# Two columns instead of four in the first phase of a decoder layer: sums kept in PSUM, eight ada_w buffers, the norm's root inside the modulation

## The chip, the cores and the metric

The kernel runs on one core of a Trainium2 chip. A core has five engines that run their own instruction queues and wait for each other by semaphores: TensorE (PE in the profile, its weight loads PEld), VectorE (DVE), ScalarE (ACT), GpSimd (POOL) and SyncE (SP), which issues the transfers here. The metric is the device time of one execution in microseconds.

## The reference

One layer of a hybrid decoder on 1024 prompt tokens and 64 sample tokens (8 sequences of 8), model width 2048, float32. The change concerns the first lines of the layer: the modulation is computed from the condition vectors `c` (nine rows: one prompt, eight samples), the input is normalised, scaled and shifted, and projected.

```python
mod = jax.nn.silu(c.astype(f32)) @ ada_w.astype(f32) + ada_b.astype(f32)
shift, scale, gate = jnp.split(mod, 3, axis=-1)
h = (_rmsnorm(x, norm_g).astype(f32) * (1.0 + scale[:, None]) + shift[:, None]).astype(dt)
proj = h @ w_in
...
vn = _rmsnorm(v_b, sgu_g)
```

`_rmsnorm` multiplies by the reciprocal root of the mean square over the 2048 features of a token. `v_b` is four columns of 128 of the projection ("vb" below). What follows (dilated attention, a spatial-gating MLP, an mLSTM, an output projection, a gated residual) is not touched.

## The kernel before

Everything lies transposed: a tile is 128 features (partitions) by 1088 tokens. There are 16 feature tiles `xs[k]`, and a column of the projection is 128 outputs by all tokens, summed over the 16 feature tiles. Tokens are cut into three chunks `CH` of 384, 384 and 320 columns, so that a product fits one PSUM bank.

Float32 products are made of three float32r products: a high and a low half of the activation (`hH`, `hL`) and of the weight (`wh`, `wl`): `hH*wh + hL*wh + hH*wl` (function `products`, lines 252 to 254). The weight's halves are made by `Weights`: SP loads `wraw`, ACT rounds it to `wh` (L98), POOL subtracts (L99). Those of a feature tile are made by `modulate` (x times scale plus shift on DVE, L420 to L424; ACT rounds it to `hH`, L425) and `modulate_low` (`hL`, L431). Before that `scaled` has multiplied x by the root `rbc` of its token (L398, on DVE for the first two tiles, on POOL for the others).

The scale and shift come from ada_w, 2048 by 6144, read in the same phase. PE multiplies it with the nine condition vectors: a group `g` of 4 MB (eight transfers of 512 KB) gives scale and shift of two feature tiles, in four sets of matmuls (`ada_set`, L342); the four row strips of the result are copied by ACT (L366, `ada_sum`), turned by PE transposes (L374, `ada_turn`) and summed by DVE (L376), and `modulation` makes scale and shift of it (L409 to L411). Group 0 is cut in two halves (`ada_half`, L353), one for each feature tile, so that the first tile comes early. Groups 8 to 11 make the gate of the residual later.

The order is written out by hand. Instructions stand in each engine's queue in the order in which Python issues them; generators such as `ada_group` are stepped between the products by tables of steps (`AT`). Buffers come from pools with a fixed number of turns. The first phase computes the four vb columns (`NST = 4`): for each feature tile or pair of tiles, the products of all four columns go to PSUM, and are added to `accs` in SBUF (by ACT's copy for the first tile, by DVE after that, L553 and L584). ada_w has four buffers of 512 KB (`ad`), of which a set takes two. Then comes the gate column (two 32-wide strips for the mLSTM's gates, L632 to L636), and from there `column` computes one column after the other, all 16 feature tiles in a row, with its sums in three PSUM banks.

PSUM has eight banks: four for products (`mm`), four for everything else (`bgp`, through `bank`).

## Time and profile before

| | us |
|---|---|
| median of three runs | 2462.2 (2461.33 to 2462.92) |
| the profiled execution | 2462.13 |
| its span in the profile | 2460.1 |
| PE busy in the span | 2419.0 |
| first vb product (its hL part) starts | 49.4 |
| gate column starts (vb columns done on PE) | 198.5 |
| DMA moved in the first 320 us, GB/s | 230 |

The profile is one execution; times in it are from the span's start. A row of the timeline has start, duration, engine, line, operation, output and inputs by their names in the program, shapes, and in brackets how long the engine was idle before it and who released it. A row of a group has the count, then busy us and the mean in ns. A row of stages has the stretch, its length, busy us and number of instructions of PE, PEld, DVE, ACT and POOL, the granted clock of PE (1.00 is full), the mean share of the DMA engines and GB/s.

### The profile page before, as it was taken

The page shows a single profiled execution, that of the slowest core. Times are in us where ns is not written, and L with a number is a line of the kernel's source. Part 1 is how long each engine was busy: PE and PEld are TensorE (multiplying, and loading weights), DVE is VectorE, ACT ScalarE, POOL GpSimd, SP SyncE. Part 2 cuts the span into 40 slices and gives each one's busy share as a digit, 9 for nine tenths or more (in the row PEclk, how much of TensorE's full clock was granted, in tenths as well). Part 3 has the DMA queues.
Part 4 walks back from the last instruction along what each step waited for, and adds up shares of the span by engine and source line. Part 5 has one row for each costly group of instructions (what it writes and reads, how often), then busy time and mean ns, then how long its engine had stood idle before and what let it go on. Part 6 is the DMA issues. An engine that isn't in the chain of part 4 may idle for free.

```text
span 2460.1 us, 39820 instructions
## 1 busy us (share of the span) xinstructions
PE 2419.0 (98%) x15879; PEld 2237.5 (91%) x15879; DVE 923.8 (38%) x2489; ACT 746.1 (30%) x1638; POOL 644.3 (26%) x502
## 2 busy tenths in 40 slices
PE   5899999999999999999999999999999999999999
PEld 2677899999999999999999999888989999999898
DVE  5662300323232231323352001333311688887322
ACT  3222221323323232323321111222212566666210
POOL 2431222232322232222221322121211333332321
PEclk8999999999999999999999999999999999999999
DMA  8774621111121112112411524657565855554454
GB/s 289 255 258 158 220 65 44 57 62 57 54 65 58 53 49 73 38 52 71 127 56 59 172 76 171 223 178 265 188 240 187 255 157 165 152 151 139 164 171 141
DMA packets 157081, 332.95 MB, mean 135 GB/s; under 512 B 21770, under 2 KB 76834, under 8 KB 149216
## 3 DMA queue, kind: packets, MB, share of 16 engines
q1 hardware_dynamic: 156896, 330.41, 41.1%
q8 instruction: 125, 2.05, 0.3%
q14 instruction: 60, 0.49, 0.1%
HBM read 284.26 MB, written 54.55 MB: 138 GB/s over the span
## 4 chain that ended last, share of the span: by engine, by line
PE 95%; DMA 2%; DVE 2%; issue 0%; SPq 0%; ACT 0%; POOL 0%; DVEq 0%; POOLq 0%; ACTq 0%
PE mm L252 27%; PE mm L254 26%; PE mm L253 26%; PE pt L1493 2%; PE ad L342 2%; PE os L1300 1%; PE o L1504 1%; PE sq L1250 1%; PE o L1502 1%; DMA ad<-in_adaw 1%; PE s L1452 1%; PE s L1451 1%; DMA x<-in_xT 1%; PE b L942 0%; PE b L974 0%; PE b L982 0%
## 5 line engine op out<-in xcount | busy, mean ns | idle before, releaser
L252 PE MATMUL mm<-hH,wh 128*128 128x384 f32 (+1 forms) x3168 | 1058.5, 334 | 9.3 <-ACT hH L425 8.1
L253 PE MATMUL mm<-hL,wh 128*128 128x384 f32 (+1 forms) x3168 | 1034.8, 327 | 2.6 <-DVE hL L431 2.6
L254 PE MATMUL mm<-hH,wl 128*128 128x384 f32 (+1 forms) x3168 | 1036.0, 327 | 0.0
L99 POOL TENSOR_TENSOR wl<-wraw,wh 128x512 fp32r<-128x512 f32 x344 | 445.7, 1304 | 1545.8 <-ACT wh L98 1433.4
L252 PEld LDWEIGHTS mm<-hH,wh 128*128 128x128 f32 x3168 | 595.9, 188 | 51.3 <-issue 32.1
L253 PEld LDWEIGHTS mm<-hL,wh 128*128 128x128 f32 x3168 | 596.3, 188 | 4.4 <-DVE hL L431 3.6
L254 PEld LDWEIGHTS mm<-hH,wl 128*128 128x128 f32 x3168 | 595.4, 188 | 0.0
L98 ACT CAST wh<-wraw 128x512 fp32r<-128x512 f32 x344 | 200.8, 596 | 409.6 <-PE mm L253 270.9
L252 PE MATMUL mm<-yH,wh 128*128 128x512 f32 (+2 forms) x768 | 261.7, 341 | 0.0
L254 PE MATMUL mm<-yH,wl 128*128 128x512 f32 (+2 forms) x768 | 251.7, 328 | 0.4 <-POOL wl L99 0.4
L253 PE MATMUL mm<-yL,wh 128*128 128x512 f32 (+2 forms) x768 | 251.7, 328 | 0.0
L254 PEld LDWEIGHTS mm<-yH,wl 128*128 128x128 f32 x768 | 144.8, 189 | 11.7 <-POOL wl L99 0.9
L252 PEld LDWEIGHTS mm<-yH,wh 128*128 128x128 f32 x768 | 145.1, 189 | 9.6
L253 PEld LDWEIGHTS mm<-yL,wh 128*128 128x128 f32 x768 | 145.3, 189 | 9.3
L898 DVE SCALAR_TENSOR_TENSOR u<-R,cw,u 128x384 f32<-128x384 f32 (+1 forms) x108 | 62.0, 574 | 213.3 <-ACT u L896 210.8
L1588 DVE SCALAR_TENSOR_TENSOR xo<-mm,gate,xo 128x512 f32<-128x512 f32 (+2 forms) x96 | 54.5, 569 | 117.4 <-PE mm L254 101.8
L1494 ACT CAST pH<-pt 128x512 fp32r<-128x512 f32 (+1 forms) x120 | 65.3, 544 | 63.3 <-PE pt L1493 62.5
L1495 DVE TENSOR_TENSOR pL<-pt,pH 128x512 fp32r<-128x512 f32 (+1 forms) x120 | 74.8, 623 | 11.6 <-ACT pH L1494 11.2
L1463 ACT ACTIVATE P<-P,mx 128x128 f32<-128x128 f32 (+3 forms) x96 | 74.4, 777 | 1.0 <-DVE mx L1460 1.0
L1493 PE MATMUL pt<-cst,P 128*128 128x128 f32 x432 | 66.6, 272 | 0.0
L1454 DVE CUSTOM_DVE_ANT_0 P<-s,btab 128x384 f32<-128x384 f32 (+2 forms) x96 | 54.7, 570 | 30.0 <-PE s L1452 29.1
L1504 PE MATMUL o<-pL,vh 128*64 128x256 f32 x240 | 61.8, 281 | 1.9 <-DVE pL L1495 1.9
(324 smaller groups left out, 2378.8 us busy)
## 6 DMA issues: line engine op xcount, KB each, us to landing
wraw<-in_win SPq DMA_DIRECT2D x264, 256.0 KB
ad<-in_adaw SPq DMA_DIRECT2D x96, 512.0 KB
kv<-in_ck SPq DMA_DIRECT2D x30, 1024.0 KB
kv<-in_cv SPq DMA_DIRECT2D x30, 1024.0 KB
wraw<-in_wout SPq DMA_DIRECT2D x48, 256.0 KB
x<-in_xT SPq DMA_DIRECT2D x16, 544.0 KB
yraw<-yD SPq DMA_DIRECT2D x16, 544.0 KB
xo<-in_xT SPq DMA_DIRECT2D x16, 544.0 KB
```

The lines of the kernel that those rows point to most:

```text
L98: self.nc.scalar.copy(wh[:, :n], raw[:, :n])
L99: self.nc.gpsimd.tensor_tensor(wl[:, :n], raw[:, :n], wh[:, :n].bitcast(FT), op=OP.subtract)
L252: T.matmul(ps[:, :n], wh[:, a], rh[:, t0:t0 + n], start=first and i == 0, stop=False)
L253: T.matmul(ps[:, :n], wh[:, a], rl[:, t0:t0 + n], start=False, stop=False)
L254: T.matmul(ps[:, :n], wl[:, a], rh[:, t0:t0 + n], start=False, stop=last and i == len(rows) - 1)
L898: V.scalar_tensor_tensor(u[:, :npr], R[:, j:j + npr], cw[:, m, j:j + 1], u[:, :npr], op0=OP.mult, op1=OP.add)
L1454: V.tensor_tensor_reduce(s[:, k0:k0 + w], ps[:, :w], e["bt"][:, x:x + w], 1.0, mx[:, np_ - 1:np_] if np_ else -3.0e38, op0=OP.add, op1=OP.max,
L1463: S.activation(s[:, :nk], s[:, :nk], AF.Exp, bias=mx[:, 2:3], accum_out=mx[:, 3:4])
L1493: T.transpose(pt[:, o:o + 128], P[r][:, k:k + 128], ident)
L1494: S.copy(pH[:, f:], pt[:, f:])
L1495: at(0, 3, lambda: V.tensor_tensor(pL[:, f:], pt[:, f:], pH[:, f:].bitcast(FT), op=OP.subtract))
L1504: T.matmul(po[0][0:64, :256], e["vh"][:, kb, 0, :], pL[:, c], start=False, stop=(kb == 2 * m + 1), skip_group_check=True)
```

## The change

The first phase now computes only the first two vb columns (`NST = 2`). Their sums over all 16 feature tiles stay in six PSUM banks (two columns by three chunks); the two other banks serve `ad` and `at`. At the end ACT copies the six sums out (`h_vb`), and the other two vb columns are computed by `column` behind the phase, with the gate column after them. ada_w has eight buffers in the phase. Groups 0 and 1 are both cut into halves, so tiles 0 to 3 come one by one, each chunk by chunk; group 2 is stepped in tile 3, and from then group g+1 in the products of group g. The multiplication by the root is gone as a step: `modulate` multiplies x by scale and root in one three-operand instruction on DVE, ACT adds the shift as it rounds to `hH`, and `modulate_low` adds the shift again on DVE as it subtracts. The first weight tile's low half is made by DVE instead of POOL.

```diff
 def bank(name="bg"):
+    if start:
+        tag = "bg" if name in ("ad", "at") else "acc"
+        return bgp.tile([128, 512], FT, tag=tag, name=name, bufs=2 if tag == "bg" else 6)
     return bgp.tile([128, 512], FT, tag="bg", name=name, bufs=4)
...
-    NST = 4
+    NST = 2
...
+    def ahead():
+        ada_dma(used[0] + (8 if start else 4))
...
-        V.tensor_scalar(x[:, a], x[:, a], md[:, 1, 0:1], md[:, 0, 0:1], op0=OP.mult, op1=OP.add)
+        V.scalar_tensor_tensor(x[:, a], x[:, a], md[:, 1, 0:1], rbc[:, a], op0=OP.mult, op1=OP.mult)
+        S.activation(hH[k][:, a], x[:, a], AF.Identity, bias=md[:, 0, 0:1])
         if t1 == TOK:
...
+            V.tensor_tensor(x[:, NPR:], x[:, NPR:], rbc[:, NPR:], op=OP.mult)
...
-        S.copy(hH[k][:, t0:t1], x[:, t0:t1])
+            S.copy(hH[k][:, NPR:], x[:, NPR:])
...
-        eng.tensor_tensor(hL[k][:, t0:t1], xs[k][:, t0:t1], hH[k][:, t0:t1].bitcast(FT), op=OP.subtract)
+        V.scalar_tensor_tensor(hL[k][:, a], xs[k][:, a], md[:, 0, 0:1], hH[k][:, a].bitcast(FT), op0=OP.add,
+                               op1=OP.subtract)
...
+    accs = [[bank("mm") for c in range(3)] for j in range(NST)]
+    for k in range(KT):
+        g, r = divmod(k, 2)
+        if r == 0:
+            wh, wl = W.get(k > 0)
+        if k == 1:
+            W.split_to(1)
+        for u in range(6):
+            c, j = divmod(u, NST)
+            t0, n = CH[c]
+            o = 256 * j + 128 * r
+            products(accs[j][c], n, wh[:, o:], wl[:, o:], [(hH[k], hL[k])], t0, k == 0, k == KT - 1)
+            if k < 3:
+                if u < 5:
+                    next(halves[k + 1])
+            elif k == 3:
+                if u % 2 == 0:
+                    next(groups[2])
+            elif g < 7:
+                x = 6 * r + u
+                if x in (0, 2, 4, 6, 8, 9, 10, 11):
+                    next(groups[g + 1])
+            if k == KT - 1:
+                h_vb(j)(c, accs[j][c], t0, n)
+            age()
+        if k < 3:
+            for c in range(3):
+                high(k + 1, c)
+                low(k + 1, c)
+        elif k == 3:
+            for _ in range(5):
+                next(groups[2])
+    flush()
+    start = False
...
+    gate_weights()
+    for g in range(NST, GB):
+        column(col["vb", g], h_vb(g))
     gate_column()
```

A unit below is the three products of one column, one chunk and one feature tile. In the changed program `products` is at lines 260 to 262, `ada_half` at L366, `ada_set` at L355, the turn at L387, the scaling at L431, ACT's shift at L432 and the low half at L445.

**Between a group's turn and the next group, PE.** Before, in the steady state, the turn of a group (`at_849`, for tiles `hH_860` and `hH_874`) is followed by products of the tiles at hand (`hH_711`, `hH_724`):

```order
L374 MATMUL at_849<-cst_86,at_829 128x128 x2
L374 MATMUL at_849<-cst_86,at_830 128x128 x2
L252 MATMUL mm_866<-hH_711,wh_591 128x320
L253 MATMUL mm_866<-hL_737,wh_591 128x320
L254 MATMUL mm_866<-hH_711,wl_592 128x320
L252 MATMUL mm_866<-hH_724,wh_591 128x320
L253 MATMUL mm_866<-hL_747,wh_591 128x320
L254 MATMUL mm_866<-hH_724,wl_592 128x320
L252 MATMUL mm_885<-hH_711,wh_686 128x384
```

Of those there are 42 until the first that reads `hH_860`, with two sets of the group after it (L342) in between. Now, with the turn `at_724` for tiles `hH_735` and `hH_751`:

```order
L387 MATMUL at_724<-cst_80,at_715 128x128 x2
L260 MATMUL mm_334<-hH_644,wh_480 128x384
L261 MATMUL mm_334<-hL_651,wh_480 128x384
L262 MATMUL mm_334<-hH_644,wl_481 128x384
L260 MATMUL mm_332<-hH_644,wh_480 128x320
L261 MATMUL mm_332<-hL_651,wh_480 128x320
L262 MATMUL mm_332<-hH_644,wl_481 128x320
L260 MATMUL mm_335<-hH_644,wh_480 128x320
L261 MATMUL mm_335<-hL_651,wh_480 128x320
L262 MATMUL mm_335<-hH_644,wl_481 128x320
L260 MATMUL mm_330<-hH_735,wh_486 128x384
L261 MATMUL mm_330<-hL_745,wh_486 128x384
```

Nine products of the tiles at hand stand between the turn and the first product of the new tile.

**The same place on DVE.** Before, scale and shift of a tile (`x_114`) are one instruction, and the adds to `accs` (L584) stand between the steps:

```order
L376 TENSOR_REDUCE ads_854<-at_849 128x36
L409 TENSOR_TENSOR md_856<-ads_854,cst_86 128x2x9
L410 TENSOR_TENSOR md_856<-ads_854,cst_86 128x2x9
L411 SCALAR_TENSOR_TENSOR md_856<-md_856,cst_86 128x2x9
L420 TENSOR_SCALAR x_114<-x_114,md_856 128x1024
L423 TENSOR_TENSOR x_114<-x_114,md_856 128x64
L424 TENSOR_TENSOR x_114<-x_114,md_856 128x64
L584 TENSOR_TENSOR acc1_232<-acc1_232,mm_866 128x320
L420 TENSOR_SCALAR x_116<-x_116,md_856 128x1024
```

Now (tiles `x_115` and `x_117`):

```order
L389 TENSOR_REDUCE ads_729<-at_724 128x36
L419 TENSOR_TENSOR md_731<-ads_729,cst_80 128x2x9
L420 TENSOR_TENSOR md_731<-ads_729,cst_80 128x2x9
L421 SCALAR_TENSOR_TENSOR md_731<-md_731,cst_80 128x2x9
L431 SCALAR_TENSOR_TENSOR x_115<-x_115,md_731,rbc_226 128x1024
L435 TENSOR_TENSOR x_115<-x_115,md_731 128x64
L436 TENSOR_TENSOR x_115<-x_115,rbc_226 128x64
L437 TENSOR_TENSOR x_115<-x_115,md_731 128x64
L445 SCALAR_TENSOR_TENSOR hL_745<-x_115,md_731,hH_735 128x1024
L448 TENSOR_TENSOR hL_745<-x_115,hH_735 128x64
L431 SCALAR_TENSOR_TENSOR x_117<-x_117,md_731,rbc_226 128x1024
```

The low half of the first tile, which waits for ACT, now stands ahead of the second tile's scaling, and the adds are gone.

**The first ada_w transfers, SP.** Before, four transfers, two weight tiles, then each further one behind a buffer that comes free. Now, with eight buffers, the row of the first ones reads:

```order
L335 DMA ad_141<-in_adaw 128x4x256
L87 DMA wraw_143<-in_win 128x2x256
L335 DMA ad_231<-in_adaw 128x4x256
L335 DMA ad_233<-in_adaw 128x4x256
L335 DMA ad_235<-in_adaw 128x4x256
L335 DMA ad_237<-in_adaw 128x4x256
L335 DMA ad_262<-in_adaw 128x4x256
```

`ad_262` is the ninth and the first that waits for a buffer.

## The prediction

> **What bounds the kernel now.** I read the page's busy shares and chain first, then the first 200 us cut into stages, since the change touches nothing else.

> ```profile
> PE 2419.0 (98%) x15879; PEld 2237.5 (91%) x15879; DVE 923.8 (38%) x2489; ACT 746.1 (30%) x1638; POOL 644.3 (26%) x502
> ...
> PE 95%; DMA 2%; DVE 2%; issue 0%; SPq 0%; ACT 0%; POOL 0%; DVEq 0%; POOLq 0%; ACTq 0%
> ```

> TensorE (PE) is the bound: it is idle for 41.1 us of the span of 2460.1 us. Work that moves from one place to another on PE therefore costs nothing in itself; only PE's waiting, and the clock that it gets, can change the time. The stages say where it waits:

> ```profile
> 0.00:47.00 47.00, 23.24 (x167) 6.48 (x167) 22.29 (x29) 14.51 (x19) 10.33 (x10) 0.94 0.95 333
> 47.00:94.00 47.00, 38.45 (x197) 24.09 (x197) 25.48 (x49) 13.73 (x33) 23.17 (x17) 0.88 0.61 206
> 94.00:198.50 104.50, 103.20 (x644) 82.71 (x643) 75.77 (x150) 23.36 (x35) 41.70 (x21) 1.00 0.70 251
> ```

> The third number is PE's busy time, the last three are the granted clock, the share of the DMA engines and GB/s. Until 47 us PE does only norm and modulation work and DMA is full; until 94 us it lacks 8.6 us; from 94 us until the four vb columns are done it lacks 1.3 us in 104.5. So four columns per feature tile are just enough work to hide the making of the next tiles. The question is whether two are.

> **The price of a column, and the point of no change.** The two weight tiles of the last feature group, and the first row of the gate column behind them:

> ```profile
> 192.58 0.34 PE L252 MATMUL mm<-hH,wh 128*128 128x384 f32 x1
> ...
> 195.56 0.34 PE L252 MATMUL mm<-hH,wh 128*128 128x384 f32 x1
> ...
> 198.54 0.34 PE L632 MATMUL mm<-hH,ifw 128*64 128x384 f32 x1
> ```

> One column times two feature tiles (18 matmuls) takes 2.98 us, so a column takes 8 x 2.98 = 23.8 us. The change leaves two columns for later, 47.7 us at full pace. The gate column starts at 198.5 us now; the changed phase breaks even if it ends 47.7 us earlier, at 150.9 us. In it, six units (two columns, three token chunks, one tile) take 2.98 us, 0.5 us each.

> **The start: the root inside the modulation.** Removed are two multiplies x*rbc on DVE and fourteen on POOL (L398). Up to the root's last step all stays in place, since the x loads stand first in SP's queue as before.

> ```profile
> 34.25 0.17 DVE L225 SCALAR_TENSOR_TENSOR rs<-rs,rs 128x9 f32<-128x9 f32 x1
> 34.48 1.86 PE L295 MATMUL rb<-cst,rs 128*128 128x128 f32 x9 [1.75 <-DVE rs L225]
> 39.67 0.64 PE L353 MATMUL ad<-ad,csp 128*32 128x256 f32 x8 [0.63 <-DMA ad<-in_adaw]
> 40.24 0.44 PE L374 MATMUL at<-cst,at 128*128 128x128 f32 x2
> 41.50 10.23 POOL L398 TENSOR_TENSOR x<-x,rbc 128x1088 f32<-128x1088 f32 x4
> 41.67 2.33 DVE L411 SCALAR_TENSOR_TENSOR md<-md,cst 128x9 f32<-128x9 f32 x1
> 49.43 0.69 PE L253 MATMUL mm<-hL,wh 128*128 128x384 f32 x1 [1.52 <-DVE hL L431]
> ```

> A nine-wide step of 0.17 us took 2.33 us beside POOL's multiplies (L411), and DVE lost about 2 us in each of the next three steps as well. That goes. The new place of the turn: two of the three rb blocks (1.86/3 = 0.62 us each) and one half set (0.64) after 34.48 us, at 36.4; scale ready 1.6 us later, 38.0. The prices of the new forms come from the nearest rows:

> ```profile
> L909 DVE SCALAR_TENSOR_TENSOR qT<-t,u 128x384 f32<-128x384 f32 x12 | 6.7, 559 | 7.5 <-ACT t L908 7.5
> L1131 DVE SCALAR_TENSOR_TENSOR vr<-vr,cst,rb 128x1088 f32<-128x1088 f32 x4 | 5.7, 1432 | 0.0
> L1463 ACT ACTIVATE P<-P,mx 128x1024 f32<-128x1024 f32 x12 | 13.8, 1154 | 0.0
> L1463 ACT ACTIVATE P<-P,mx 128x384 f32<-128x384 f32 x12 | 7.3, 611 | 1.0 <-DVE mx L1460 1.0
> ```

> Scale-and-root 0.56 us (L909's form), ACT's shift 0.61 (L1463, which also has a bias per partition), low half 0.56; the first weight's low half, moved from POOL to DVE, fits beside ACT. The first hL product starts at 39.9 us instead of 49.43: a gain of 9.5 us.

> **Tiles 0 to 3.** Each tile now has a half of its own: four sets on PE, one behind each of the first four units, then copy, turn, scale, chunk by chunk. From the last half set: copy and gaps 0.55, turn to scale 1.6, 0.56 + 0.65 + 0.56 and gaps: 4.05 us to the next tile's first hL product. Then four units (2.0) and four half sets (0.6 each, 2.4): 8.4 us a tile. The last half set of tile 1 ends at 39.9 + 4.4 = 44.3, that of tile 3 at 61.1; tile 3's products and three sets of group 2, its last set and copies follow. For the sets of groups:

> ```profile
> 98.16 1.92 PE L342 MATMUL ad<-ad,csp 128*32 128x512 f32 x16
> 100.01 0.42 PE L252 MATMUL mm<-hH,wh 128*128 128x320 f32 x1
> ```

> These are two sets, 1.85 us (the row before is of such a pair in one go), 0.93 each. 61.1 + 4.05 + 3.0 + 2.8 + 0.9 + 0.8 puts the turn of group 2 at 72.6 us.

> **Groups: a chain in place of a cover.** In steady state before:

> ```profile
> 93.60 0.60 PE L374 MATMUL at<-cst,at 128*128 128x128 f32 x4
> ...
> 95.19 0.81 DVE L420 TENSOR_SCALAR x<-x,md 128x1024 f32<-128x1024 f32 x1
> ...
> 98.30 1.28 DVE L431 TENSOR_TENSOR hL<-x,hH 128x1088 fp32r<-128x1088 f32 x1
> ```

> From the turn to the scaling 1.6 us; then the new form, 1024 wide. Its price lies between 1.2 us (the two-input L431, 1.28 x 1024/1088) and 1.35 (L1131, 1.43 x 1024/1088); I take 1.2, since L909 lies on that slope. ACT 1.15 plus 0.1, the low half 1.2 and gaps 0.15: the first low product of the next group can start 5.4 us after the turn. Before, 42 matmuls of the old group and two sets stood behind the turn, 42 x 0.166 + 1.85 = 8.8 us; now nine matmuls do, 1.5 us. PE runs dry 1.95 us behind the turn and waits for 3.4 us, with one high product in it. Then nine units (4.5) and four sets (3.7) until the next turn: 13.6 us a group, where PE has 10.1 us of work. Five of them put the turn of group 7 at 140.6. Its second tile's low half comes 9.4 us after the turn (5.4 + 0.2 + 1.2 + 1.25 + 1.2 and gaps) and six units follow: the phase ends 12.4 us later, at 153.0.

> Removed with the PSUM sums are 12 adds a tile on DVE (hidden now, so nothing is gained), and POOL has one weight split a group instead of two; the split of tile 2 can meet the chain as in L411's row, 1 us once. The switch of pools waits for the vb copies of the last two banks, 0.6 us; ada_w of group 8, without a head start, is issued when the vb columns end, a gate column (15 us) before its use, so 0.

> **Eight buffers.** The DMA engines' rows:

> ```profile
> 22.00:26.00 4.00, 2.64 (x21) 0.45 (x18) 1.87 (x2) 1.58 (x2) 0.00 (x0) 1.00 1.02 408
> 30.00:32.00 2.00, 1.39 (x17) 0.64 (x7) 0.00 (x0) 0.89 (x2) 0.00 (x0) 1.00 1.11 349
> 48.00:50.00 2.00, 0.57 (x2) 0.50 (x2) 2.00 (x2) 0.00 (x0) 2.00 (x2) 0.50 0.00 0
> 102.00:106.00 4.00, 3.74 (x24) 2.60 (x26) 2.57 (x6) 0.00 (x0) 4.00 (x2) 1.00 1.02 414
> ```

> Four buffers left the DMA idle (48 to 50 us). With eight, a half (2.1 MB in 1 KB rows) needs 6.0 us at 349 GB/s and a group with its weights (4.45 MB) 10.9 us at 410: less than 8.4 and 13.6, so the chain binds, not the DMA.

> **The clock.** What waits of this length do:

> ```profile
> 69.10 1.11 PE L374 MATMUL at<-cst,at 128*128 128x128 f32 x4 [2.33 <-ACT at L366]
> ...
> 69.87 0.67 PE L252 MATMUL mm<-hH,wh 128*128 128x384 f32 x1
> ...
> 72.68 0.34 PE L252 MATMUL mm<-hH,wh 128*128 128x384 f32 x1
> ...
> 80.51 0.41 PE L252 MATMUL mm<-hH,wh 128*128 128x384 f32 x1 [2.62 <-ACT hH L425]
> ```
> ```profile
> 70.00:71.00 1.00, 1.00 (x6) 1.00 (x5) 0.68 (x4) 0.00 (x0) 0.00 (x0) 0.50 1.05 422
> 80.00:81.00 1.00, 0.49 (x3) 0.52 (x4) 1.00 (x3) 0.98 (x2) 1.00 (x2) 1.00 0.00 0
> ```

> After one wait of 2.3 us the granted clock was 0.50 and nine matmuls took 2.81 us, 1.3 us more than at 0.166 us each; after another of 2.6 us it stayed at 1.00. The six waits of group 2 to 7 are longer (3.4 us, the first 5). A loss lies between 0 and about 2.7 us each (5.4 us of work at half clock); I take 1.5, nearest to the 1.3 measured, and 1.5 once more for the start, where PE is less busy than before at 36 to 38 us. That is 10.5 us. [...]

> **Sum.** 153.0 - 150.9 = 2.1, plus 1 and 0.6, plus 10.5: 14.2 us. The profiled execution took 2462.13 us (span and 2.0 us around it; the median of three is 2462.2): 2476 us, 0.58% slower. About 0.2% (4.9 us) is what a measurement can tell from no change.

> **Rivals.**
> The clock holds: the waits fall across two of its periods of judgement, as the one at 80.51 did. Then +3.7 us, 2466: no change. Against it stand six longer waits. 0.14.
> The chain is hidden or shorter, and the DMA sets the pace of 10.9 us: 5 x 2.7 = 13.5 us less and no clock loss, 2452, faster. It decides once a group takes less than 13.6 - 3.7/5 = 12.9 us; that asks for 0.7 us off a chain whose steps are priced from rows, and for a full clock. For it speaks only that my 9.5 us at the start may be short. 0.12.
> The DMA keeps the pace of the last stage above, 251 GB/s: 17.7 us a group, 5 x 4.1 more with half of the clock loss, some 2491. Against it: those 251 are starved by four buffers, with 414 in between. 0.08.
> That the order is not what the diff says is excluded by the built program.

> The forecast itself has 0.66. Range 2461 to 2490: from the clock holding, with a start better by 5 us, to all six waits at 2.7 us and 1 KB rows slowing the tiles. Faster 0.13, same 0.16, slower 0.71.

> **What would show it.** The first hL product near 40 us; turns of the groups 13.6 us apart, or 15 with the clock; in each, a PE wait of about 3.4 us that ends at DVE's hL (L445), with a clock of 0.5 in stretches up to 160 us; the first two columns done at 153 to 164 us; the gate column at 201 to 213. Wrong would be: groups 11 us apart with DMA above 400 GB/s, waits that end at ada_w, or a loss behind the gate column.

## The result, and the profile after

The changed kernel takes 2491.9 us (median of four runs, 2490.3 to 2494.0) against 2462.6 for the kernel before in the same comparison: a ratio of 1.0120 (95% interval 1.0102 to 1.0137), 29.4 us slower. The forecast was 14.2 us slower, with a range of 2461 to 2490 us: the direction was right, the size was half of what came, and the measured time lies above the range. The profiled execution took 2493.99 us.

The three stages of the changed kernel, by the same view as before (PE's busy time third; granted clock, DMA share and GB/s last). The last one ends with the vb columns, at 227 us instead of 198.5:

```profile
0.00:47.00 47.00, 27.89 (x195) 9.14 (x195) 18.61 (x41) 15.90 (x22) 0.73 (x5) 0.96 1.00 352
47.00:94.00 47.00, 36.88 (x202) 17.34 (x203) 21.45 (x55) 11.99 (x24) 5.53 (x4) 0.82 0.82 282
94.00:227.00 133.00, 118.97 (x643) 91.38 (x643) 42.32 (x81) 28.92 (x55) 18.81 (x13) 0.87 0.47 160
```

Up to 47 us PE does more than before (27.9 us busy against 23.2). In the two later stages it is idle for 24 us, and the granted clock is 0.82 and 0.87, where the kernel before had 0.88 and 1.00. The DMA engines are busy for 0.82 and 0.47 of these stages; whether PE waits for them is read from its waits, below.

One group in detail, and the ends of the phase, from the timeline of PE (start, duration, operation, in brackets how long PE stood idle before it and what released it):

```profile
38.89 0.44 PE L261 MATMUL mm<-hL,wh 128*128 128x384 f32 x1 [0.21 <-DVE hL L445]
...
113.65 0.60 PE L387 MATMUL at<-cst,at 128*128 128x128 f32 x4
...
117.66 0.65 PE L260 MATMUL mm<-hH,wh 128*128 128x384 f32 x1 [2.02 <-ACT hH L432]
118.98 0.69 PE L261 MATMUL mm<-hL,wh 128*128 128x384 f32 x1 [0.67 <-DVE hL L445]
...
130.73 0.60 PE L387 MATMUL at<-cst,at 128*128 128x128 f32 x4
...
179.36 0.45 PE L260 MATMUL mm<-hH,wh 128*128 128x384 f32 x1 [0.57 <-ACT vb L546]
...
226.99 0.34 PE L631 MATMUL mm<-hH,ifw 128*64 128x384 f32 x1
```

The reader should see three things (a high product reads `hH`, a low product `hL`). The first low product starts at 38.89 (forecast 39.9). From the turn at 113.65 to the group's first low product it is 5.33 us (forecast 5.4). From there to the next turn, at 130.73, it is 11.75 us, where the forecast had 8.2. The turns of groups 2 to 7 stand at 79.38, 96.58, 113.65, 130.73, 147.80 and 164.89: 17.1 us apart.

What happens in those 11.75 us shows in a table of stretches of 3.413 us, laid where the granted clock steps. In this trace it steps twenty times between 39.2 and 175.8 us, from 1.00 to 0.50 or back, and two steps that follow each other lie 3.413 us or two or three times that apart. A stretch of this grid is a window in what follows. First one group's period, then one tile's:

```profile
97.26:100.67 3.41, 1.40 (x10) 1.13 (x8) 2.67 (x9) 1.27 (x2) 0.00 (x0) 1.00 0.95 317
100.67:104.09 3.42, 2.74 (x11) 0.87 (x11) 3.11 (x6) 0.87 (x2) 0.00 (x0) 0.50 0.49 195
104.09:107.50 3.41, 3.41 (x14) 1.99 (x14) 2.50 (x2) 0.94 (x3) 1.72 (x1) 0.50 0.50 112
107.50:110.91 3.41, 3.41 (x26) 1.70 (x19) 0.00 (x0) 0.00 (x0) 0.00 (x0) 1.00 0.93 304
110.91:114.33 3.42, 3.42 (x24) 2.30 (x24) 0.04 (x1) 0.65 (x2) 0.00 (x0) 1.00 0.97 356
```
```profile
59.71:63.13 3.42, 3.42 (x21) 1.22 (x19) 2.31 (x8) 2.00 (x5) 0.03 (x1) 0.50 0.30 103
63.13:66.54 3.41, 3.41 (x30) 1.82 (x27) 0.00 (x0) 0.79 (x2) 2.50 (x2) 1.00 0.32 80
66.54:69.95 3.41, 1.52 (x9) 0.99 (x8) 2.26 (x7) 0.61 (x1) 0.00 (x0) 1.00 0.95 326
```

A group takes exactly five such windows (17.07 us): one at full clock with PE busy for only 1.40 us, two at half clock, two full ones. Its first window at half clock has the 0.7 us wait for the low half in it (2.74 us busy), the second is busy throughout. A tile takes exactly three (10.24 us), one of them at half clock. The sum of PE's waits in the first 230 us:

```profile
PE mm L260 <- ACT hH L432: 20.5, 10, 3.4
...
PE mm L261 <- DVE hL L445: 4.6, 9, 0.7
```

No wait for ada_w stands in that list, whose other rows are left out here. PE waits for the chain, as forecast, and then works at half clock.

### The profile page after: what moved, and what is told of

It reads as the page before. It is cut to its first block, busy times and chain, and to the rows that moved or that the text cites. A ratio compares the mean times of both kernels' runs of the same rounds, so it can differ in the third digit from the quotient of the medians.

```text
span 2492.1 us, 39810 instructions
## 1 busy us (share of the span) xinstructions
PE 2438.3 (98%) x15911; PEld 2241.9 (90%) x15911; DVE 881.2 (35%) x2437; ACT 751.6 (30%) x1654; POOL 593.4 (24%) x478
## 4 chain that ended last, share of the span: by engine, by line
PE 95%; DMA 2%; DVE 2%; ACT 1%; issue 0%; SPq 0%; DVEq 0%; ACTq 0%
PE mm L260 26%; PE mm L261 26%; PE mm L262 26%; PE pt L1495 2%; PE ad L355 2%; PE o L1506 1%; PE o L1504 1%; PE os L1302 1%; PE sq L1252 1%; PE s L1454 1%; PE s L1453 1%; DMA x<-in_xT 1%; PE b L944 0%; PE b L976 0%; PE b L984 0%; PE b L983 0%
## 5 line engine op out<-in xcount | busy, mean ns | idle before, releaser
L108 POOL TENSOR_TENSOR wl<-wraw,wh 128x512 fp32r<-128x512 f32 (+1 forms) x343 | 439.6, 1289 | 1638.5 <-ACT wh L101 1564.3
L262 PEld LDWEIGHTS mm<-yH,wl 128*128 128x128 f32 x768 | 144.8, 189 | 10.9
L1497 DVE TENSOR_TENSOR pL<-pt,pH 128x512 fp32r<-128x512 f32 (+1 forms) x120 | 74.8, 623 | 11.1 <-ACT pH L1496 10.7
```

What stands on the lines that cost most here:

```text
L108: eng.tensor_tensor(wl[:, :n], raw[:, :n], wh[:, :n].bitcast(FT), op=OP.subtract)
L262: T.matmul(ps[:, :n], wl[:, a], rh[:, t0:t0 + n], start=False, stop=last and i == len(rows) - 1)
L1497: at(0, 3, lambda: V.tensor_tensor(pL[:, f:], pt[:, f:], pH[:, f:].bitcast(FT), op=OP.subtract))
```

## The experiments

Three theories were put against each other. Theory 1: the chain costs what was priced, and each wait costs whole windows at half clock, more than priced. Theory 2: the chain and the sets are dearer than priced, with the clock a bystander. Theory 3: transfers, or the weights in SP's queue ahead of them, set the pace. Each ratio below is against the kernel before, run beside it.

**Work in the waits.** Unread products that keep PE busy, nothing moved:

```diff
+    def warm(n, w, k):
+        ps = bank("wm")
+        for _ in range(n):
+            T.matmul(ps[:, :384], w[:, :128], hH[k][:, 0:384], start=True, stop=True)
...
+        if k < 3:
+            warm(8, wh, k)
+        if 3 < k < KT - 1 and k % 2:
+            warm(11, wh, k)
...
-            for _ in range(5):
+            for i in range(5):
                 next(groups[2])
+                if i == 1:
+                    warm(17, wh, k)
```

> The changed kernel with matrix products whose results nobody reads, put where TensorE stands before the high product: 8 of 128x384 behind the last unit of each of tiles 0 to 2, 17 behind the turn of group 2, 11 behind the eighth unit of each later group (0.167 us each at full clock, so 1.8 us into a wait of 3.4 us). Nothing else moves. Theory 1 (each wait costs two whole windows of 3.41 us at half clock, on top of the chain): the clock holds at 1.00 over the groups, their turns come about 13.7 us apart instead of 17.07, tiles 8.5 us apart instead of 10.26, and the time is 2468 to 2474 us against 2491.9. Theory 2 (the chain from the turn to the low product and the sets' work are dearer than priced, clock or not): TensorE ends the added work inside its waits, the turns stay 17 us apart, 2490 to 2494 us. Theory 3 (the ada_w transfers or the weight transfers ahead of them in SP's queue set the pace): also 17 us, 2490 to 2494 us, and the waits move to the transfers.

Measured: 2472.7 us, ratio 1.0034 (1.0023 to 1.0046), and in the profiled execution (2469.9 us, the fastest of the six) a mean granted clock of 1.000. Tiles come 8.8 us apart (8.5 expected), groups 14.6 (13.7 expected). PE's timeline of this run, two turns, and a set between two units:

```profile
102.50 0.60 PE L387 MATMUL at<-cst,at 128*128 128x128 f32 x4
...
104.33 2.10 PE L560 MATMUL wm<-hH,wh 128*128 128x384 f32 x11
106.52 0.44 PE L260 MATMUL mm<-hH,wh 128*128 128x384 f32 x1
107.84 0.45 PE L261 MATMUL mm<-hL,wh 128*128 128x384 f32 x1 [0.88 <-DVE hL L445]
...
110.19 0.33 PE L261 MATMUL mm<-hL,wh 128*128 128x384 f32 x1
110.36 0.34 PE L262 MATMUL mm<-hH,wl 128*128 128x384 f32 x1
110.63 1.06 PE L355 MATMUL ad<-ad,csp 128*32 128x512 f32 x8
111.63 0.45 PE L260 MATMUL mm<-hH,wh 128*128 128x384 f32 x1
111.91 0.34 PE L261 MATMUL mm<-hL,wh 128*128 128x384 f32 x1
...
117.11 0.60 PE L387 MATMUL at<-cst,at 128*128 128x128 f32 x4
```

The kernel does more work and is 21 us faster than the changed one by the ratios. From the turn to the low product it is still 5.34 us, so the chain is the same; the period falls from 17.07 to 14.61 us. That is theory 1, and it leaves a rest: 14.61 is 1 us above the forecast's 13.6. The rows of the set show it. Without a set, a product follows the one before by 0.17 us (the rows at 110.19 and 110.36); with one, the next starts 1.27 us later and its successor 0.28 after that. A set alone displaces 1.27 - 0.17 + 0.11 = 1.2 us, not the 0.93 that the forecast took as half of two sets in one go. Four of them make 1.1 us a group.

**The same in the groups alone.**

> The same unread products in the groups alone (17 behind the turn of group 2, 11 behind the eighth unit of the later groups), none in tiles 0 to 2. Theory 1: the tiles keep their 10.26 us, the groups come down to 13.7 us; five periods of 3.4 us and group 2's own windows are gone, 2472 to 2477 us, and the difference to the run with all of them (3 to 6 us) is what half clock costs in the tiles. Theories 2 and 3: 2490 to 2494 us.

Measured: 2477.0 us, ratio 1.0052 (1.0037 to 1.0067); tiles at 10.3 us, groups at 14.6. So half clock costs 4.3 us in tiles 0 to 3 (2477.0 - 2472.7) and the rest in the groups.

**Fewer of them.**

> The changed kernel with the unread products in the groups alone, and fewer: 5 instead of 11 (0.9 us instead of 1.9 into a wait of 3.4), and 11 instead of 17 behind the turn of group 2. The waits left are 2.4 us and a last one of 0.9. It tells where the clock falls. If a wait of that length is too short: as with 11 of them, 14.6 us a group and 2476 to 2479 us. If it is long enough: 17.07 us a group as without any, 2490 to 2494 us; a mixture would show periods of both lengths.

Measured: 2482.2 us, ratio 1.0072 (1.0055 to 1.0089): the mixture. Between the turns lie 14.7, 14.6, 16.2, 14.6 and 16.2 us. The waits are alike in all groups, and the table of windows shows why some fall and some do not:

```profile
95.55:98.96 3.41, 2.75 (x19) 2.42 (x16) 2.62 (x8) 0.74 (x1) 0.00 (x0) 1.00 0.97 388
98.96:102.38 3.42, 2.09 (x12) 0.74 (x12) 2.95 (x5) 0.88 (x3) 0.00 (x0) 1.00 0.74 298
102.38:105.79 3.41, 3.41 (x24) 2.13 (x28) 2.76 (x4) 1.47 (x3) 1.73 (x1) 1.00 0.67 197
...
112.62:116.03 3.41, 1.40 (x9) 0.63 (x11) 2.78 (x7) 1.28 (x2) 0.00 (x0) 1.00 0.98 393
116.03:119.44 3.41, 3.41 (x14) 1.79 (x8) 2.78 (x6) 1.80 (x3) 0.92 (x1) 0.50 0.26 51
119.44:122.86 3.42, 3.42 (x24) 1.30 (x23) 0.90 (x1) 0.00 (x0) 0.81 (x1) 1.00 0.96 320
```

In the upper rows an edge of the window cut the same 2 us of idle time in two (0.66 and 1.33 us), and the clock stayed at 1.00; in the lower ones all of it lay in one window (1.40 us busy), and the next window was at 0.50. That one was busy throughout, and only one was lost.

**Filling only the short wait.** The 0.7 us between the high and the low product, which lies in the first window at half clock:

```diff
             T.matmul(ps[:, :n], wh[:, a], rh[:, t0:t0 + n], start=first and i == 0, stop=False)
+            for _ in range(fill):       # 3 in the first unit of a group
+                T.matmul(wm[:, :n], wh[:, a], rh[:, t0:t0 + n], start=True, stop=True)
             T.matmul(ps[:, :n], wh[:, a], rl[:, t0:t0 + n], start=False, stop=False)
```

> The changed kernel with three unread products of 128x384 between the first high product of a group and the low product behind it, where TensorE waits 0.7 us; the long wait ahead of the high product is left as it is. In the changed kernel the window behind the long wait (2.74 of 3.41 us busy) runs at half clock and so does the one behind that. If a window at half clock has to be busy throughout for the clock to come back, filling the 0.7 us gives back the second one: 1.7 us a group from group 3 on and for group 2, six in all, 2480 to 2485 us, with one window at 0.50 a group. If a fall lasts two windows whatever is done in them, the added products can only cost: 2490 to 2496 us.

Measured: 2484.7 us, ratio 1.0084 (1.0067 to 1.0100), 9 us faster than the changed kernel by the ratios. One of its groups, in windows:

```profile
116.65:120.07 3.42, 1.42 (x6) 0.94 (x6) 2.79 (x7) 1.28 (x2) 0.00 (x0) 1.00 1.02 413
120.07:123.48 3.41, 3.41 (x14) 1.65 (x14) 2.78 (x6) 1.80 (x3) 0.68 (x1) 0.50 0.30 85
123.48:126.89 3.41, 3.41 (x25) 1.49 (x24) 1.12 (x1) 0.00 (x0) 1.04 (x1) 1.00 0.92 321
```

The window behind the fall is now busy throughout (3.41 us, where the six falls of the changed kernel's groups have 2.72 to 2.78), and the next is at 1.00. So here a wait of 0.7 us, short in itself, was what cost the second window. In this profile group 2 still lost two (the window behind its fall was busy for 3.16 us, not throughout), and one group lost none.

**The waits taken away by order.** The sets of a group by its second unit and the turn behind the fourth, so that eight units stand behind a turn instead of three:

```diff
-                if x in (0, 2, 4, 6, 8, 9, 10, 11):
+                for _ in range({0: 2, 1: 2, 3: 1, 5: 1, 7: 1, 9: 1}.get(x, 0)):
                     next(groups[g + 1])
```

> The changed kernel with its groups' steps at other units: all four sets of a group by the second unit (two steps at unit 0, two at unit 1), the turn behind unit 3, so that eight units stand between a turn and the first product that needs it instead of two or three. No operation is added or removed. Theory 1: eight units are about 4.5 us, the wait of 3.4 us falls to some 1 us, too short for the clock to fall, and the groups come about 11.1 us apart, near the 10.9 us of their transfers: 2459 to 2466 us, which is no slower than the kernel before. Theory 2 (chain alone, no clock): only the 2.4 us of wait that the units cover go, five times 2.4 us: 2478 to 2482 us. Theory 3 (transfers set the pace): the sets, now earlier, wait for their transfers and the turns stay 17 us apart, 2490 to 2494 us.

Measured: 2464.6 us, ratio 1.0002 (0.9992 to 1.0011). Moving steps alone gives back all of the 29 us; the clock is 1.00 from 95 us on, and from group 3 on the turns come 11.5 to 12.3 us apart (11.1 expected). The time is theory 1's.

**The same for tiles 0 to 3 and group 2.**

```diff
-                if u < 5:
+                for _ in range({0: 2, 1: 2, 2: 1}.get(u, 0)):
                     next(halves[k + 1])
             elif k == 3:
-                if u % 2 == 0:
+                for _ in range({0: 2, 1: 1, 2: 1, 3: 1}.get(u, 0)):
                     next(groups[2])
```

> The run with the groups' steps moved (2464.6 us), and the same done to tiles 0 to 3: a tile's half sets behind its first two units instead of one behind each of five, so that three units stand between a turn and the product that needs it; group 2's sets by the second unit of tile 3 and its turn behind the fourth. Theory 1 (the wait's length sets the clock): the wait per tile falls from 1.7 to about 0.7 us, a tile runs at full clock and takes 8 to 8.8 us instead of 10.3, group 2's wait loses 2 us and its half-clock windows; together 6 to 10 us, unless the transfers (348 GB/s, busy for 0.99 of the first 62 us) become the bound: 2454 to 2460 us. Theory 3 for this stretch (transfers at their pace): TensorE waits for ada_w instead, 2462 to 2467 us.

Measured: 2457.7 us, ratio 0.9973 (0.9962 to 0.9984), faster than both kernels. The longest wait left is one of 2.54 us, at the end of tile 3, with two windows at half clock behind it; from group 3 on the groups run at full clock, 11.5 to 11.7 us apart. From its timeline and its windows:

```profile
75.58 0.44 PE L260 MATMUL mm<-hH,wh 128*128 128x384 f32 x1 [2.54 <-ACT hH L432]
```
```profile
96.00:132.00 36.00, 33.80 (x226) 22.48 (x223) 25.13 (x49) 11.87 (x23) 5.24 (x4) 1.00 0.92 357
```

Two further steps from there, each on that last wait:

> The run before this one in the list with unread matrix products in its remaining waits: 4 of 128x384 behind tiles 0 to 2 and 12 behind tile 3. Theory 1: where the wait alone is now too short for the clock to fall, nothing is gained, and the time is within 2 us of that run; where a fall is left (group 2's wait at the end of tile 3 is the likeliest), it goes: 2452 to 2458 us. Theory 3: the same as that run, since the transfers set the pace.

> The run with all steps moved earlier (2457.7 us), and with it the groups' first tile modulated in three pieces. Theory 1: what is left there is one wait of 2.5 us at the end of tile 3 with two windows at half clock, and 0.9 us per group for the low half; the pieces take 1.9 us off the first and its windows go (some 3.4 us more); the groups gain nothing where their transfers already set the pace of 11.5 us. 2451 to 2456 us, faster than the kernel before by 0.3 to 0.5%. Theory 3 (transfers at their pace from start to end of the phase): 2456 to 2459 us.

Measured: 2457.6 us (0.9967, 0.9954 to 0.9980) and 2456.8 us (0.9969, 0.9957 to 0.9982). Both take the fall at the end of tile 3 away (clock 1.00 from 75 to 95 us) and neither is measurably faster than without. The DMA engines are busy for 0.99 and 1.00 of the time from 40 to 95 us in the two runs, as theory 3 would have it, but PE hardly waits for them: between 40 and 135 us its list of waits has none for ada_w in the first run and 0.5 us in the second. The transfers run ahead into the eight buffers. In the second run it is PE's own work that sets the pace of the groups, 11.0 us from group 3 on at full clock:

```profile
90.00:130.00 40.00, 40.00 (x267) 25.62 (x257) 32.54 (x75) 16.07 (x34) 6.93 (x4) 1.00 0.88 345
```

Part of the gain may be spent again: the first run has 24 added products (4 us of PE's time at 0.167 us each), and the second loses one window to the clock behind the last group, at 138.8 us. Neither was tested by itself.

**A shorter chain in the changed order.** The first tile of a group in three pieces, as `high` and `low` do it for tiles 0 to 3 (the second of the two runs above has this edit too):

```diff
-                modulate(2 * g + k, md[k])
+                for t0, n in CH if k == 0 else ((0, TOK),):
+                    modulate(2 * g + k, md[k], t0, t0 + n)
+                    if k == 0:
+                        modulate_low(2 * g, md[0], t0, t0 + n)
                 yield
-                modulate_low(2 * g + k, md[k])
+                if k:
+                    modulate_low(2 * g + k, md[k])
```

> The changed kernel with the first tile of each group modulated in three pieces of 384, 384 and 320 elements (high and low half of a piece together), as tiles 0 to 3 are, instead of one of 1024. The order of TensorE's work stays. By the rows of tiles 0 to 3 (0.62 us for a piece on VectorE, 0.61 on ScalarE, 0.62 for its low half) the first low product can start 3.5 us behind the turn instead of 5.3. Theory 1: the waits shrink to about 1.3 us, the clock holds over the groups, and a group takes 12.5 to 13 us instead of 17.07; with tiles 0 to 3 unchanged, 2464 to 2470 us. Theory 2 (chain alone): only the 1.9 us go, 15.2 us a group, 2480 to 2484 us. Theory 3: no change, 2490 to 2494 us.

Measured: 2474.9 us, ratio 1.0045 (1.0030 to 1.0060). The mechanism is theory 1's: the first low product comes 3.5 us behind the turn, and the clock holds from group 3 to group 7. The size is missed by 5 us. A group takes 13.3 us, not 12.5 to 13: from its low product to the next turn it is 9.8 us, 0.5 more than with the clock held and one piece, and part of that is a new wait for the second tile's low half, which now comes later on DVE. From PE's timeline:

```profile
97.60 0.44 PE L261 MATMUL mm<-hL,wh 128*128 128x384 f32 x1 [0.21 <-DVE hL L445]
...
104.72 0.44 PE L261 MATMUL mm<-hL,wh 128*128 128x384 f32 x1 [0.29 <-DVE hL L445]
...
107.42 0.60 PE L387 MATMUL at<-cst,at 128*128 128x128 f32 x4
```

Besides, one window each was still lost to the clock in group 2 and behind the last group, at 153 us.

**Parts of the change undone, and one alone.** First four ada_w buffers instead of eight (`bufs=4`, `ahead` by four):

> The changed kernel with four ada_w buffers in the first phase instead of eight, which undoes that part of the change. Theory 1: a period of 17.07 us holds 10.9 us of transfers, but with four buffers only two of a group's four sets can lie ready, so the last two wait for transfers: slower by 0 to 4 us a group, 2492 to 2512 us. Theory 3 in its stronger form (eight buffers let ada_w transfers crowd out others): faster, 2480 to 2490 us.

Measured: 2509.2 us, ratio 1.0178 (1.0160 to 1.0197). Turns 18.2 to 19.6 us apart, and PE's list of waits now has transfers in it:

```profile
PE ad L366 <- DMA ad<-in_adaw: 4.1, 1, 4.1
PE ad L355 <- DMA ad<-in_adaw: 2.6, 8, 0.6
```

The eight buffers are worth about 14 us in this order (1.0178 - 1.0120), more than the waits for transfers alone (6.7 us). In the profiled execution 19 windows of the first 200 us are at half clock, against 16 in the changed kernel.

Then the root multiplied beforehand again:

> The changed kernel with one of its parts undone: x is multiplied by the norm's root beforehand again, tiles 0 and 1 on VectorE, the others on POOL, and the modulation is one multiply-and-add on VectorE and a copy on ScalarE as before; the low halves stay on VectorE. By the forecast's first step the part is worth the 10 us by which the first product came earlier (38.9 against 49.4): 2496 to 2504 us. Rival: the multiplies by the root only filled time that the first phase waits away in any case, and the shorter VectorE step (0.81 us for 1024 elements in the kernel before, 1.28 now) takes 0.5 us out of each group's chain: 2486 to 2494 us.

Measured: 2505.5 us (2498.0 to 2507.1), ratio 1.0164 (1.0147 to 1.0180), 11 us slower than the changed kernel by the ratios. In sum the part is worth about what the forecast's first step gave it, but the sum has two terms. In the profiled execution of this run (2498.0 us, the fastest of the four) the turn of group 2 comes at 94.29 us instead of 79.38, 14.9 us later; the five group periods behind it then take 78.5 us together instead of 85.5. The chain is no shorter, as the rival had it: from the turn at 125.78 to the low product at 131.12 it is 5.34 us. But only four windows of these periods are at half clock, against ten in the changed kernel. Two rows of PE and one of POOL from this run show where:

```profile
46.61 0.69 PE L260 MATMUL mm<-hH,wh 128*128 128x384 f32 x1 [8.41 <-ACT hH L439]
51.69 0.69 PE L261 MATMUL mm<-hL,wh 128*128 128x384 f32 x1 [4.40 <-DVE hL L445]
```
```profile
38.73 12.49 POOL L411 TENSOR_TENSOR x<-x,rbc 128x1088 f32<-128x1088 f32 x4 [37.41 <-ACT rbc L305]
```

The first low product waits until 51.69 us while POOL multiplies.

And the root inside the modulation alone, in the kernel before (four columns, sums in SBUF, four buffers):

> The kernel before with one part of the change alone: the norm's root inside the modulation (POOL's multiplies of x by the root are gone, VectorE does the low halves), still four columns and four buffers. All theories: the first low product comes some 8 to 10 us earlier than at 49.43 us, as in the changed kernel (38.9). By the forecast's steps those 9.5 us are worth keeping: 2452 to 2458 us. Rival: the tiles of the kernel before are paced by the transfers or by the chain, which is now longer by the low halves on VectorE, and the gain is given back by the end of the columns: 2460 to 2470 us.

Measured: 2474.5 us (2467.6 to 2478.3), ratio 1.0037 (1.0022 to 1.0051), slower, and outside both expectations. The first low product is early (44.2 us, though not the 39 to 41 expected), and the gain is more than given back in the groups, which take up to 20.3 us where the kernel before took at most 17.4. From 94 to 200 us, PE's longest wait is one that the kernel before does not have there:

```profile
PE mm L252 <- DVE acc L583: 9.4, 10, 1.3
```

In that kernel DVE also adds the products to `acc`, and the longer modulation (1.28 us instead of 0.81 for 1024 elements) stands ahead of the adds that free PSUM banks; two windows with 1.6 us of work lost their clock as well. So the root inside the modulation did not pay without the rest of the change. That it is the sums in PSUM that make the room on DVE is argued from these rows; no run has the two without the other parts.

## What the prediction had right, and the step that failed

- **The point of no change.** 150.9 us for the end of the two columns. They end at 178.8 (the next column starts at 179.36, after the 0.57 us of the pool switch, forecast 0.6): 27.9 late, the gate column is 28.45 us late, the median time 29.4. Right as a measure. (The two profiled executions are 31.9 us apart, 3.5 of it behind the gate column's start. That stretch lasts 2261.0 to 2265.1 us in the fourteen traces, 2261.6 in that of before and 2265.1 in that of the changed kernel; what varies it stays open.)
- **The start.** 38.89 instead of 39.9: right. That undoing the part costs 11 us, near the 9.5, is partly luck: in the profiled execution of that run it is 14.9 us until the turn of group 2, less 7.0 us in the groups behind it, where fewer windows ran at half clock.
- **The chain in the groups.** Turn to low product 5.33 us (5.4), waits of 2.02 and 0.67 us with one product between them (3.4 in all). Right.
- **The sets.** Mis-sized: 0.93 us each, taken from two in one go; one alone displaces 1.2. With the clock held, group 2 turns at 73.20 (72.6) and the groups are 14.64 us apart on average (13.6): 0.6 + 5 x 1.04 = 5.8 us of the miss.
- **The clock: the step that failed.** "I take 1.5" for each of six waits and 1.5 for the start, 10.5 us. Against the run with the clock held, the changed kernel loses 6.2 us until the turn of group 2 (79.38 against 73.20), 5 x 2.46 us in the groups and 1.5 us behind the last turn (164.89 to 178.8, against 146.42 to 158.8): 20.0 us. That is 9.5 us of the miss. With the 5.8 above, less 1 us of DVE beside POOL that was priced and did not come onto the path (L448 took 1.30 us beside a weight split, and nobody waited for it), it makes 14.3 of the 15.2 us. Two things were wrong in the step. In the groups each wait cost two windows, not part of one (a window of 3.413 us at 0.50 loses 1.7 us of work): six falls lost 13.8 us, 2.3 each (less than twice 1.7, since PE waits in part of the first window), where 9.0 were priced. The 1.5 came from a single fall, behind which PE had no second wait (3.3 of 3.41 us busy in the window at 0.50); the upper bound of 2.7 us, from 5.4 us of work at half clock, was the author's estimate, and no row gives it. And the falls in tiles 1 to 3 got no price, and no reason for that: their waits of 1.7 us are shorter than the 2.3 behind which the clock had fallen, but a window that holds one has only 1.52 us of work, and all three fell, 4.4 us together. The fall at the start was priced and came, 1.5 us.
- **Eight buffers and the DMA.** "The chain binds, not the DMA": right for this order (no wait for ada_w in the changed kernel), and in the re-ordered runs the DMA does not bind either. Their groups take 11.0 to 11.8 us on average from group 3 on, near the 10.9 priced for the transfers, but PE waits for ada_w for 0.5 us at most in them.
- **The rivals.** "The clock holds" has its wait cut by an edge in two traces. In that of the kernel before, the clock steps at 68.98 and 72.39 us; two windows on, an edge at 79.22 cuts the wait from 77.89 to 80.51, the windows on both sides of it have 2.0 and 2.1 us of work, and the clock stayed at 1.00. In the run with fewer products it stayed where the parts were 0.66 and 1.33 us. But in the changed kernel none of the ten waits, from the start to group 7, was spared by it: the clock fell behind each. "The chain is hidden, and the DMA sets the pace" did not happen in this order. In the runs with moved steps the chain is nearly hidden, but PE's own work sets most of the pace; the 2452 us were 5 below the best of them (2456.8). "The DMA keeps the pace of 251 GB/s" gave 17.7 us a group and 2491, close to the 17.07 and 2491.9 measured. That is luck: PE has no wait for ada_w, and with the same transfers and PE kept busy a group takes 14.6 us.

## What to carry to other kernels

In these traces the clock fell behind windows of 3.413 us with 1.71 us of work or less, and a wait of 0.7 us behind a fall kept it at 0.50 for a second window. Where TensorE is the bound and the trace shows its clock fall like that, price a wait by the windows it empties, not by its length: count PE's work within each, and count the short waits behind a fall too. Before taking work out of a loop that hides a chain, move the chain's start ahead of what is left: the same change with its steps moved went from 1.2% slower to 0.3% faster. And price a short batch between other products as it will stand, alone (a set displaced 1.2 us here), not as half of a pair (0.93).

## What the runs showed of the hardware

In the changed kernel the rounds locked to these windows: 10.3 us a tile and 17.07 us a group are three and five of them, the same in every round, where the same work at full clock took 8.8 and 14.6. Other orders did not all lock. With fewer added products, with only the short wait filled and with the root multiplied beforehand, rounds of 14.6 us stand beside some of 15.8 to 17.7, and with four buffers a group takes 18.2 to 19.6 us. Why the changed kernel falls into whole windows was not tested. Added work that nobody reads, 1.9 us a group, and some in the tiles, made the kernel 21 us faster.
